# Adding the last two experts' rows after the final norm instead of before it, in a routed feed-forward block on one Trainium2 core

## The chip, the cores and the metric

The program runs on one core of a Trainium2 chip. The metric is device microseconds (us) of one execution, less being better. TensorE is called PE, VectorE DVE, ScalarE ACT, GpSimd POOL; SyncE (SP) and POOL issue the DMAs spoken of here.

## What is computed

The reference is one layer (a convolution and recurrence mixer, a cross-attention, a mixture of experts) and a final norm. Only its end matters here:

```python
def rms_norm(x, g):
    y = x * lax.rsqrt(jnp.mean(x * x, axis=-1, keepdims=True) + 1e-6)
    return y * g

# 1024 tokens of 1024 numbers; 16 experts in 4 groups of 4
# a token takes ONE group, and two experts of that group
for e in range(16):
    hid = silu(t @ w_gate[e]) * (t @ w_up[e])          # 1024 -> 512
    out = out + combine[:, e:e+1] * (hid @ w_down[e])  # 512 -> 1024
x = x + out
return rms_norm(x, final_norm)                         # row by row
```

## The kernel before

Float32 products are made of three products of the high and low parts of both operands, so every weight tile is split once: a cast on ACT (`split_hi`, L163) and a subtraction on DVE (`split_lo`, L169).

**Routing.** `idi` and `wts` hold, for every expert, the token numbers and gates of its first 128 rows (`slot(e, 0)`) and of up to 64 further rows (`slot(e, 1)`). Blank places hold numbers of 1024 and more, which the scatters skip. What the further rows need stands under `second(e)`, a branch on a flag of the expert, taken by PE, ACT and DVE. `ORDER` runs through the groups in turn, so that the last two experts, `p` and `LAST` (numbers 11 and 15), belong to different groups: no token has both. In the run profiled here the flag is set for `p`, not for `LAST`.

**The sum.** `acd` is a DRAM copy of the residual rows. An expert's rows are added to it by an indirect accumulating DMA from POOL (`add_rows`, L1200), first rows and further rows apart. Each such DMA touches `acd` at places that the program doesn't know when it is built, so each waits until the one before has landed.

**The weights.** `Weights` (`X`) streams the tiles. Nine raw slots take loads from SP, in the order in which W was filled; `X.split(n)` splits up to n tiles into free slots out of 14 pairs, and each split frees a raw slot and issues the next load. `X.get` splits until the wanted tile is there. All of this part is in `manual_schedule`: every engine runs its instructions in the order of the code.

**The loop** (L1323) takes expert `e`: gate and up products (`gate_up`, L1327, 48 matmuls of 128x512), `hidden`, the down products of the expert before (`down`, 24 matmuls), its scaled rows (`weighted`, L1148) and scatter-add, `over` (turns the hidden rows for the next down product), the further rows of the expert before, `over2`, `turned2`.

**The tail** (L1368 to L1425) has the down products of `p`, its two scatter-adds, the gate and up products of `LAST`, its `hidden`, reads of all eight 128-row tiles of `acd` (L1403, SP), and the down products of `LAST`.

**The final phase** (L1429 to L1484) places the rows of `LAST` by matmuls with one-hot matrices (L1437, L1443). Even tiles (mode A) are added on DVE (L1450), squared on ACT (L1459), and scaled on DVE (L1467). In odd tiles (mode B) a matmul with the identity adds the residual (L1445), ACT squares out of PSUM (L1456), DVE scales (L1470). POOL makes the reciprocal root (L1457, L1460, L1461), SP stores each tile (L1475).

Of the kernel before, what the change touches and what calls it, by code (L numbers as in the profile page):

```python
# [8 lines left out]
F32 = mybir.dt.float32  # L9
F32R = mybir.dt.float32r  # L10
# [43 lines left out]
C_N = C_WR + ND * 24  # L54


MODES = "ABABABAB"
START = 12
FILL = 2
LAG = 2  # L60


class Slots:
# [22 lines left out]
def block_kernel(ctx: ExitStack, tc: tile.TileContext, A):  # L86
# [572 lines left out]
    for s, e in enumerate(ORDER):  # L659
        gu = [("gu", e, k) for k in range(ND)]  # L660
        dn = [("dn", ORDER[s - 1], k) for k in range(4)] if s else []
        for name, i, k in dn + gu if s == NE - 1 else gu + dn:
            W.add((name, i, k), A["w_" + name][i, k])
    for k in range(4):
        W.add(("dn", ORDER[-1], k), A["w_dn"][ORDER[-1], k])
# [541 lines left out]
    def second(e):  # L1207

        return tc.If((flags & (1 << e)) > 0, preferred_fallthrough_block=True)

    hrow = [half.get() for _ in range(2)]
    routed = half.get(BF16, (P, P))
    act.copy(routed, idf)
# [98 lines left out]
    with tc.manual_schedule():  # L1312
        flags = nc.values_load(two[0:1, 0:1], engines=(PE, ACT, DVE), min_val=0, max_val=(1 << NE) - 1)
        X = Weights(W.jobs, W.flying, W.ready, RAW)
        X.load()
        x0 = x0_bufs[0]
        run(turned(x0, xg[0]))
        with second(ORDER[0]):
            turned2()
        for i in range(2):  # L1320
            fetch(ORDER[1], i)
        pool.memset(og[1][LO], 0.0)
        for s, e in enumerate(ORDER[:-1]):  # L1323
            p = ORDER[s - 1] if s else None
            nx = ORDER[s + 1]
            for k in range(ND):
                gate_up(x0, X.get(("gu", e, k)), k)  # L1327
                X.split(1)
            hidden()
            ws = [X.get(("gu", e, k)) for k in range(ND)]  # L1330
            with second(e):
                for k in range(ND):
                    gate_up2(ws[k], k)
                hidden2(slot(e, 1)[1])
            for k in range(ND):
                X.drop(("gu", e, k))
            x0 = x0_bufs[(s + 1) % 2]
            ops = turned(x0, xg[0])
            if s + 2 < NE:
                fetch(ORDER[s + 2], 0)  # L1340
            run(ops)
            X.split(2)
            if p is not None:
                wd = [X.get(("dn", p, k)) for k in range(4)]
                for k in range(4):
                    down(wd[k], k)
                X.split(1)
                weighted(slot(p, 0)[1])
                add_rows(slot(p, 0)[0], og[0])
            over()  # L1350
            X.split(2)
            if p is not None:
                with second(p):
                    for k in range(4):
                        down2(wd[k], k)
                    rows2(og[1])
                add_rows(slot(p, 1)[0][LO], og[1][LO])
                for k in range(4):
                    X.drop(("dn", p, k))
            with second(e):  # L1360
                over2()
            with second(nx):  # L1362
                turned2()
            if s + 2 < NE:
                fetch(ORDER[s + 2], 1)


        p, LAST = ORDER[-2:]  # L1368
        wd = [X.get(("dn", p, k)) for k in range(4)]
        for k in range(4):  # L1370
            down(wd[k], k)
        X.split(1)
        weighted(slot(p, 0)[1])
        add_rows(slot(p, 0)[0], og[0])
        with second(p):
            for k in range(4):
                down2(wd[k], k)
            rows2(og[1])
        add_rows(slot(p, 1)[0][LO], og[1][LO])
        for k in range(4):  # L1380
            X.drop(("dn", p, k))
        slots.put(*xg, *x0_bufs[NE % 2])
        fn, row = slots.get(), slots.get()
        oh = slots.get(F32R), slots.get(F32R)
        pool.iota(row, pattern=[[1, T]], base=0, channel_multiplier=0, allow_small_or_imprecise_dtypes=True)
        pool.dma_start(fn, A["final_norm"])
        for k in range(ND):
            gate_up(x0, X.get(("gu", LAST, k)), k)
            X.split(2)
        hidden()  # L1390
        ws = [X.get(("gu", LAST, k)) for k in range(ND)]
        with second(LAST):
            for k in range(ND):
                gate_up2(ws[k], k)
            hidden2(slot(LAST, 1)[1])
        for k in range(ND):
            X.drop(("gu", LAST, k))
        assert not X.jobs
        X.split(4)
        wd = [X.get(("dn", LAST, k)) for k in range(4)]  # L1400
        acc = [X.place(X.raw, F32) for _ in range(NT)]
        for t in range(NT):
            sp.dma_start(acc[t], acd[cut(t), :])  # L1403
        over()
        with second(LAST):
            over2()
        slots.put(*x0, xp)
        slots.free.extend(X.raw)
        ogs = [[slots.get(F32R) for _ in range(2)] for _ in range(2)]
        for i in range(2):  # L1410
            dve.tensor_scalar(oh[i], row, idf[:, LAST * 8 + i:LAST * 8 + i + 1], None, op0=ALU.is_equal)
        with second(LAST):
            for k in range(4):
                down2(wd[k], k)
            rows2(og[1])
            split(ogs[1][0][LO], ogs[1][1][LO], og[1][LO])
        for k in range(4):
            down(wd[k], k)
        for n in range(2):
            split(ogs[0][0][:, HS[n]], ogs[0][1][:, HS[n]], dn_banks[n], slot(LAST, 0)[1])  # L1420
        for k in range(4):
            X.drop(("dn", LAST, k))
        slots.free.extend(X.pair)
        slots.put(*og, hid, hp)
        banks.put(*gu_banks, *dn_banks, *turn_banks)  # L1425

    ssf = const.tile([P, 2 * NT], F32, name="ssf")  # L1429
    rf = const.tile([P, NT], F32, name="rf")  # L1430
    pss, jk = {}, {}

    def placed(t):
        jk[t] = slots.get()
        pss[t] = [banks.get() for _ in range(2)]
        for n, ps in enumerate(pss[t]):
            pe.matmul(ps, oh[0][:, cut(t)], ogs[0][0][:, HS[n]], start=True, stop=False)  # L1437
        with second(LAST):
            for n, ps in enumerate(pss[t]):
                for o in ogs[1]:  # L1440
                    pe.matmul(ps, oh[1][LO, cut(t)], o[LO, HS[n]], start=False, stop=False)
        for n, ps in enumerate(pss[t]):
            pe.matmul(ps, oh[0][:, cut(t)], ogs[0][1][:, HS[n]], start=False, stop=MODES[t] != "B")  # L1443
            if MODES[t] == "B":
                pe.matmul(ps, ident, acc[t][:, HS[n]], start=False, stop=True)  # L1445

    def added(t):
        if MODES[t] != "B":
            for n, ps in enumerate(pss[t]):
                dve.tensor_tensor(acc[t][:, HS[n]], ps, acc[t][:, HS[n]], op=ALU.add)  # L1450

    def summed(t):
        r, s2 = rf[:, t:t + 1], [ssf[:, 2 * t + n:2 * t + n + 1] for n in range(2)]
        if MODES[t] == "B":
            for n, ps in enumerate(pss[t]):
                act.activation(jk[t][:, HS[n]], ps, AF.Square, scale=1.0 / 32.0, accum_out=s2[n])  # L1456
            pool.tensor_scalar(r, s2[0], s2[1], EPS, op0=ALU.add, op1=ALU.add)  # L1457
        else:
            act.activation(jk[t], acc[t], AF.Square, scale=1.0 / 32.0, accum_out=s2[0])  # L1459
            pool.tensor_scalar(r, s2[0], EPS, None, op0=ALU.add)  # L1460
        pool.tensor_tensor(r, r, mhalf[:, 0:1], op=ALU.pow)  # L1461
        slots.put(jk[t])

    def scaled(t):
        r = rf[:, t:t + 1]
        if MODES[t] == "A":
            dve.scalar_tensor_tensor(acc[t], acc[t], r, fn, op0=ALU.mult, op1=ALU.mult)  # L1467
        elif MODES[t] == "B":
            for n, ps in enumerate(pss[t]):
                dve.scalar_tensor_tensor(acc[t][:, HS[n]], ps, r, fn[:, HS[n]], op0=ALU.mult, op1=ALU.mult)  # L1470
        else:
            act.activation(acc[t], acc[t], AF.Copy, scale=r)
            pool.tensor_tensor(acc[t], acc[t], fn, op=ALU.mult)
        banks.put(*pss[t])
        sp.dma_start(A["out"][cut(t), :], acc[t])  # L1475

    with tc.manual_schedule():
        for t in range(NT + LAG):
            if t < NT:
                placed(t)  # L1480
                added(t)
                summed(t)
            if t >= LAG:
                scaled(t - LAG)  # L1484


def layout(inputs):
# [63 lines left out]
```

## Time and profile before

| | |
|---|---|
| median of the runs | 1223.09 us (1222.92 to 1223.41) |
| the profiled execution | 1224.64 us, its span 1222.9 us |
| PE busy over the span | 96% |
| DVE, ACT, POOL busy | 58%, 46%, 15% |
| mean granted clock of PE | 0.988 of full speed |

A busy share is a mean over a span with several stages. The stages around the change are the last 66 us, from 1157 us on; the two loops of stages ahead of them are not touched but for the one split named below. The time of an execution is 1.7 us more than its span.

### The profile page before, as it was taken

Reading aid. Unit: us, or ns where it says so; the run is one execution under the profiler, and the core shown is the slowest. Engines: PE = TensorE matmul, PEld = TensorE weight load, DVE = VectorE, ACT = ScalarE, POOL = GpSimd, SP = SyncE. Lnnn points to the kernel's source line nnn. Section 1 sums busy time; section 2 is a strip of 40 time slices with the busy share of each in tenths; the row PEclk is TensorE's granted clock in tenths of the full one; section 3 lists DMA queues with packets and bytes.
Section 4 is the critical chain, followed back from the end, with each engine's and each line's share of the span. In section 5 each row is a group of like instructions: output and inputs, shape, how many; then the busy total and the mean of one; then the engine's idle time right before and its main releaser. Section 6 shows DMA issues by size and latency. Waiting matters only on the chain. (4 is left out here: it accounts for less than half of the span.)

```text
span 1222.9 us, 20592 instructions
## 1 busy us (share of the span) xinstructions
PE 1178.0 (96%) x7918; PEld 966.8 (79%) x7918; DVE 712.3 (58%) x1162; ACT 567.5 (46%) x965; POOL 188.6 (15%) x229
## 2 busy tenths in 40 slices
PE   9999999999999999999999999789999999999985
PEld 7787878787889988898888888568787777787762
DVE  6625454547457512364454776756867768668645
ACT  6613232323335402463244443545866767658633
POOL 1100101010100100100001333212223222123122
PEclk9999999999999999999999999889999999999988
DMA  9601110111426811120032321667979779798764
GB/s 343 240 18 48 41 54 35 36 53 54 157 85 242 281 63 35 35 104 1 1 121 83 125 104 70 218 232 242 317 245 377 254 263 349 255 338 290 247 176 194
DMA packets 58316, 196.48 MB, mean 161 GB/s; under 512 B 8925, under 2 KB 9565, under 8 KB 58208
## 3 DMA queue, kind: packets, MB, share of 16 engines
q1 hardware_dynamic: 45216, 157.69, 35.2%
q0 software_dynamic: 12704, 37.26, 10.4%
q8 instruction: 68, 1.11, 0.4%
q14 instruction: 40, 0.33, 0.1%
q10 hardware_dynamic: 288, 0.09, 0.0%
HBM read 173.49 MB, written 29.62 MB: 166 GB/s over the span
## 5 line engine op out<-in xcount | busy, mean ns | idle before, releaser
L257 PE MATMUL b<-s,s 128*128 128x512 f32 (+1 forms) x1056 | 402.7, 382 | 0.9 <-ACT s L165 0.8
L259 PE MATMUL b<-s,s 128*128 128x512 f32 (+1 forms) x1056 | 392.6, 372 | 0.0
L258 PE MATMUL b<-s,s 128*128 128x512 f32 (+1 forms) x1056 | 392.1, 371 | 0.1
L169 DVE TENSOR_TENSOR s<-s,s 128x1024 fp32r<-128x1024 f32 (+2 forms) x272 | 315.1, 1203 | 57.1 <-ACT s L163 35.4
L163 ACT CAST s<-s 128x1024 fp32r<-128x1024 f32 (+2 forms) x272 | 268.2, 1042 | 133.5 <-PE b L259 47.7
L1124 PE MATMUL b<-s,s 128*128 128x512 f32 x1152 | 275.3, 397 | 4.5 <-PEq L1362 1.7
L1124 PEld LDWEIGHTS b<-s,s 128*128 128x128 f32 x1152 | 217.0, 191 | 51.9 <-ACT s L163 2.7
L259 PEld LDWEIGHTS b<-s,s 128*128 128x128 f32 x1056 | 199.0, 188 | 35.4 <-issue 0.2
L257 PEld LDWEIGHTS b<-s,s 128*128 128x128 f32 x1056 | 199.0, 189 | 33.5 <-ACT s L165 1.5
L258 PEld LDWEIGHTS b<-s,s 128*128 128x128 f32 x1056 | 199.5, 189 | 31.3 <-DVE s L171 1.0
L169 DVE TENSOR_TENSOR s<-b,s 128x512 fp32r<-128x512 f32 (+1 forms) x112 | 70.9, 647 | 45.5 <-ACT s L163 42.5
L1200 POOL DMA_INDIRECT acd<-s,idi x30 | 59.2, 1972 | 204.9 <-ACT s L1148 66.4
L1163 PE MATMUL b<-s,s 128*128 128x512 f32 x384 | 90.5, 391 | 0.0
L1163 PEld LDWEIGHTS b<-s,s 128*128 128x128 f32 x384 | 71.6, 188 | 14.7
L163 ACT CAST s<-b 128x512 fp32r<-128x512 f32 (+1 forms) x112 | 60.7, 558 | 42.6 <-PE b L264 16.6
L1106 POOL DMA_INDIRECT s<-h3d,idi x32 | 37.1, 1160 | 106.4 <-PE b L1114 87.3
L1175 ACT COPY h<-b 64x512 f32<-64x512 f32 x32 | 18.6, 582 | 67.7 <-PE b L1163 57.0
L1176 DVE TENSOR_TENSOR h<-b,h 64x512 f32<-64x512 f32 x16 | 10.9, 682 | 63.1 <-ACT h L1175 63.1
L784 DVE TENSOR_TENSOR s<-b,s 128x512 f32<-128x512 f32 x16 | 11.0, 691 | 58.7 <-PE b L259 58.6
L264 PE MATMUL b<-ident,s 128*128 128x128 f32 x288 | 40.9, 273 | 1.0 <-DVE s L615 0.9
L547 DVE TENSOR_TENSOR s<-s,s 128x512 f32<-128x512 f32 x28 | 19.3, 691 | 37.6 <-PE b L538 22.1
L264 PEld LDWEIGHTS b<-ident,s 128*128 128x128 f32 x288 | 34.5, 140 | 8.0 <-DVE s L615 1.3
(232 smaller groups left out, 920.2 us busy)
## 6 DMA issues: line engine op xcount, KB each, us to landing
s<-in_w_gu_dram SPq DMA_DIRECT2D x128, 512.0 KB, 6.8
s<-in_w_dn_dram SPq DMA_DIRECT2D x64, 512.0 KB, 7.5
s<-in_w_in_dram SPq DMA_DIRECT2D x26, 512.0 KB, 3.5
s<-in_w_kv_dram SPq DMA_DIRECT2D x16, 512.0 KB, 5.5
h3d<-s POOLq DMA_DIRECT2D x9, 512.0 KB, 3.1
acd<-s POOLq DMA_DIRECT2D x9, 512.0 KB, 3.2
s<-in_xT_dram SPq DMA_DIRECT2D x16, 256.0 KB, 5.5
s<-in_x_dram SPq DMA_DIRECT2D x8, 512.0 KB, 9.0
```

Source lines behind the costliest of these rows:

```text
L163: act.copy(hi, src)
L169: (eng or dve).tensor_tensor(lo, src, hi.bitcast(F32), op=ALU.subtract)
L257: pe.matmul(ps, lh, rh, start=first, stop=False)
L258: pe.matmul(ps, lh, rl, start=False, stop=False)
L259: pe.matmul(ps, ll, rh, start=False, stop=last)
L264: pe.transpose(pt[:, cut(c)], src[:, cut(half * 4 + c)], ident)
L547: dve.tensor_tensor(k4[:, :, 0, :], k4[:, :, 0, :], tv[:, :, 1:2].to_broadcast([P, nb, w]), op=ALU.mult)
L1106: pool.indirect_dma_start(out=to, out_offset=None, in_=h3d, in_offset=rows, bounds_check=T - 1, oob_is_err=False)
L1124: pe.matmul(ps[n], l, r[:, HS[n]], start=a, stop=b)
L1163: pe.matmul(ps[n], l, r[:, HS[n]], start=first and i == 0, stop=last and i == 1)
L1175: act.copy(up2[UP], ps[UP])
L1200: pool.indirect_dma_start(out=acd, in_=src, in_offset=None, compute_op=ALU.add, out_offset=rows, bounds_check=T - 1, oob_is_err=False)
```

## The change

The down products of `p` move behind the gate and up products of `LAST`; the weights come in that order too. In the loop's last turn, the two splits between `over` and the second scatter-add of expert 7 are left out there, and their tiles are split later.

The rows of `p` and `LAST` are no longer added to `acd`. All eight tiles of `acd` are read as they are after expert 7 (four into free slots, four into raw slots as these come free during the products of `LAST`), normed and stored to the output: tiles 0 to 2 ahead of `over`, tiles 3 to 7 behind the further rows of `p`. The rows that `p` and `LAST` change are gathered from `acd` by four indirect DMAs of POOL. Each expert's products are added to its rows (`first_sum`, `second_sum`), the sum is normed, and stored over the output's rows by an indirect DMA (`store`), which skips blank places. Gone are the one-hot placing and its operands, the identity matmuls, and the two scatter-adds of `p`. Odd tiles change from mode B to mode C: ACT scales by the root, POOL multiplies by the norm's weights.

```diff
-MODES = "ABABABAB"
+MODES = "ACACACAC"
...
-        for name, i, k in dn + gu if s == NE - 1 else gu + dn:
+        for name, i, k in gu + dn:
...
             over()
-            X.split(2)
+            if nx != ORDER[-1]:
+                X.split(2)
...
         p, LAST = ORDER[-2:]
-        wd = [X.get(("dn", p, k)) for k in range(4)]
-        for k in range(4):
-            down(wd[k], k)
-        X.split(1)
-        weighted(slot(p, 0)[1])
-        add_rows(slot(p, 0)[0], og[0])
-        with second(p):
-            for k in range(4):
-                down2(wd[k], k)
-            rows2(og[1])
-        add_rows(slot(p, 1)[0][LO], og[1][LO])
...
+        def residual(ts):
+            for t in ts:
+                sp.dma_start(acc[t], acd[cut(t), :])
+
+        def root(r, *ss):
+            if len(ss) == 2:
+                pool.tensor_scalar(r, ss[0], ss[1], EPS, op0=ALU.add, op1=ALU.add)
+            else:
+                pool.tensor_scalar(r, ss[0], EPS, None, op0=ALU.add)
+            pool.tensor_tensor(r, r, mhalf[0:r.shape[0], 0:1], op=ALU.pow)
...
+        def scaled(t):
+            r = rf[:, t:t + 1]
+            if MODES[t] == "A":
+                dve.scalar_tensor_tensor(acc[t], acc[t], r, fn, op0=ALU.mult, op1=ALU.mult)
+            else:
+                act.activation(acc[t], acc[t], AF.Copy, scale=r)
+                pool.tensor_tensor(acc[t], acc[t], fn, op=ALU.mult)
+            sp.dma_start(A["out"][cut(t), :], acc[t])
+
+        def final(ts):
+            for i, t in enumerate(ts):
+                summed(t)
+                if i:
+                    scaled(ts[i - 1])
+            scaled(ts[-1])
...
+        def first_sum(j, e):
+            a, (r, ss) = ax[j][0], again(j, 0)
+            for n in range(2):
+                dve.scalar_tensor_tensor(a[:, HS[n]], dn_banks[n], slot(e, 0)[1], a[:, HS[n]],
+                                         op0=ALU.mult, op1=ALU.add)
+                squares(a[:, HS[n]], ss[n])
+            root(r, *ss)
+
+        def second_sum(j, e, wd):
+            a, (r, ss) = ax[j][1][LO], again(j, 1)
+            with second(e):
+                for k in range(4):
+                    down2(wd[k], k)
+                rows2(og[1])
+                dve.tensor_tensor(a, a, og[1][LO], op=ALU.add)
+                squares(a, ss[0][LO])
+            root(r[LO], ss[0][LO])
+
+        def store(ix, src):
+            rows = bass.IndirectOffsetOnAxis(ap=ix, axis=0)
+            pool.indirect_dma_start(out=A["out"], in_=src, in_offset=None, out_offset=rows,
+                                    bounds_check=T - 1, oob_is_err=False)
+
+        def first_out(j, e):
+            a, r = ax[j][0], again(j, 0)[0]
+            dve.scalar_tensor_tensor(a, a, r, fn, op0=ALU.mult, op1=ALU.mult)
+            store(slot(e, 0)[0], a)
+
+        def second_out(j, e):
+            a, r = ax[j][1][LO], again(j, 1)[0]
+            with second(e):
+                dve.scalar_tensor_tensor(a, a, r[LO], fn[LO], op0=ALU.mult, op1=ALU.mult)
+            store(slot(e, 1)[0][LO], a)
...
         for k in range(ND):
             gate_up(x0, X.get(("gu", LAST, k)), k)
-            X.split(2)
+            X.split(1)
+            if not X.jobs and len(X.raw) >= 5 and len(acc) == 4:
+                residual(range(4))
+                acc += [X.place(X.raw, F32) for _ in range(4)]
+                residual(range(4, NT))
+                fn = X.place(X.raw, F32)
+                pool.dma_start(fn, A["final_norm"])
...
         X.split(4)
-        wd = [X.get(("dn", LAST, k)) for k in range(4)]
-        acc = [X.place(X.raw, F32) for _ in range(NT)]
-        for t in range(NT):
-            sp.dma_start(acc[t], acd[cut(t), :])
+        wd, wl = ([X.get(("dn", e, k)) for k in range(4)] for e in (p, LAST))
+        slots.free.extend((*X.pair, *X.raw))
+        jk = slots.get()
+        ax = [[slots.get() for _ in range(2)] for _ in range(2)]
+        for j, e in enumerate((p, LAST)):
+            for i in range(2):
+                ix, to = (slot(e, 1)[0][LO], ax[j][1][LO]) if i else (slot(e, 0)[0], ax[j][0])
+                pool.indirect_dma_start(out=to, out_offset=None, in_=acd,
+                                        in_offset=bass.IndirectOffsetOnAxis(ap=ix, axis=0))
+        final(range(0, 3))
+        for k in range(4):
+            down(wd[k], k)
         over()
+        first_sum(0, p)
+        second_sum(0, p, wd)
         with second(LAST):
             over2()
+        final(range(3, NT))
+        first_out(0, p)
+        second_out(0, p)
+        second_sum(1, LAST, wl)
+        second_out(1, LAST)
         for k in range(4):
+            down(wl[k], k)
+        first_sum(1, LAST)
+        first_out(1, LAST)
```

## Rows read from the trace of the kernel before

**Rows 1.** The page's 40 slices of the span (30.6 us each): busy tenths of PE.

```profile
PE   9999999999999999999999999789999999999985
```

**Rows 2.** Instructions of PE in order of time, merged (start, length, line, operation, count; in brackets the idle time before and what ended it): the 48 gate and up products of expert 7, the 24 down and 16 further-row products of `p`, the 48 gate and up products of `LAST`, the turn of its hidden rows, its 24 down products.

```profile
1107.55 11.16 PE L1124 MATMUL b<-s,s 128*128 128x512 f32 x48 [0.27 <-PEq L1362]
...
1157.14 5.95 PE L1124 MATMUL b<-s,s 128*128 128x512 f32 x24 [0.42 <-ACT s L163]
...
1162.93 3.79 PE L1163 MATMUL b<-s,s 128*128 128x512 f32 x16
...
1166.56 5.60 PE L1124 MATMUL b<-s,s 128*128 128x512 f32 x24
...
1173.07 0.73 PE L1124 MATMUL b<-s,s 128*128 128x512 f32 x2 [0.91 <-ACT s L163]
...
1174.33 5.28 PE L1124 MATMUL b<-s,s 128*128 128x512 f32 x22 [0.53 <-DVE s L169]
...
1182.87 1.12 PE L1139 MATMUL b<-ident,h 128*128 128x128 f32 x4 [3.26 <-DVEq L1392]
...
1184.71 7.73 PE L1124 MATMUL b<-s,s 128*128 128x512 f32 x24 [0.72 <-ACTq L1405]
```

**Rows 3.** POOL and SP in order of time, merged: the last four scatter-adds (expert 7, first and further rows; `p`, first and further rows), and the reads of `acd`.

```profile
1156.89 2.15 POOL L1200 DMA_INDIRECT acd<-s,idi  x1 [15.51 <-ACT s L1148]
1167.85 1.43 POOL L1200 DMA_INDIRECT acd<-s,idi  x1 [8.81 <-DMA acd<-s,idi]
1171.11 1.56 POOL L1200 DMA_INDIRECT acd<-s,idi  x1 [1.82 <-DMA acd<-s,idi]
1178.00 2.12 POOL L1200 DMA_INDIRECT acd<-s,idi  x1 [5.33 <-DVE s L169]
...
1183.53 5.05 SPq L1403 DMA_DIRECT2D s<-acd  x8
```

**Rows 4.** DMA issues (KB each, median us from issue to landing), one answer for the window of each of the four scatter-adds above, in the same order; then the first two reads of `acd` and the last one; the last store of the output; a gather of 128 rows (`h3d`) at 775.5 us.

```profile
acd<-s,idi POOLq DMA_INDIRECT x1, 10.2
...
acd<-s,idi POOLq DMA_INDIRECT x1, 2.5
...
acd<-s,idi POOLq DMA_INDIRECT x1, 6.2
...
acd<-s,idi POOLq DMA_INDIRECT x1, 5.2
...
s<-acd SPq DMA_DIRECT2D x2, 512.0 KB, 6.0
...
s<-acd SPq DMA_DIRECT2D x1, 512.0 KB, 10.1
...
out_dram<-s SPq DMA_DIRECT2D x1, 512.0 KB, 2.7
...
s<-h3d,idi POOLq DMA_INDIRECT x1, 4.6
```

**Rows 5.** The final phase in order of time, merged: PE's first two one-hot products and SP's last store.

```profile
1193.00 1.07 PE L1437 MATMUL b<-s,s 128*128 128x512 f32 x2 [0.55 <-ACT s L165]
...
1215.06 0.33 SPq L1475 DMA_DIRECT2D out_dram<-s  x1
```

**Rows 6.** Splits of seven weight tiles in a row, ACT and DVE in order of time, merged; and ACT's two splits that the change takes out of the loop's last turn, and its step of `over2` of `p` behind them.

```profile
1110.42 6.75 ACT L163 CAST s<-s 128x1024 fp32r<-128x1024 f32 x7 [0.17 <-ACTq L1362]
...
1112.06 8.04 DVE L169 TENSOR_TENSOR s<-s,s 128x1024 fp32r<-128x1024 f32 x7 [0.29 <-DVEq L1362]
...
1156.96 2.03 ACT L163 CAST s<-s 128x1024 fp32r<-128x1024 f32 x2
1159.32 0.37 ACT L1157 CAST s<-b 128x256 fp32r<-128x256 f32 x1 [0.33 <-ACTq L1353]
```

**Rows 7.** Groups of instructions by line and shape (busy us, mean ns of one, idle time before and what ended it): square and its read-out on ACT, copy of 64 rows on ACT, the DVE operations that answer to those of the change, the root's two steps and a multiplication of 128x512 on POOL.

```profile
L1459 ACT ACTIVATE s<-s 128x1024 f32<-128x1024 f32 x4 | 4.2, 1057 | 7.7 <-DVE s L1450 6.0 <-issue 1.8
...
L1459 ACT ACTIVATION_READ_ACCUMULATOR s<-s 128x1 f32 x4 | 0.7, 186 | 0.0
...
L1175 ACT COPY h<-b 64x512 f32<-64x512 f32 x32 | 18.6, 582 | 67.7 <-PE b L1163 57.0 <-DVE s L1176 10.6
...
L1176 DVE TENSOR_TENSOR s<-b,h 64x512 f32<-64x512 f32 x16 | 10.9, 683 | 13.7 <-DMA acd<-s,idi 7.9 <-ACTq L1360 4.9 <-ACT h L1175 0.7
...
L1470 DVE SCALAR_TENSOR_TENSOR s<-b,rf,s 128x512 f32<-128x512 f32 x8 | 5.6, 745 | 0.8 <-POOL rf L1461 0.8
...
L1467 DVE SCALAR_TENSOR_TENSOR s<-s,rf,s 128x1024 f32<-128x1024 f32 x4 | 5.1, 1276 | 0.0
...
L961 POOL TENSOR_TENSOR s<-s,s 128x512 f32<-128x512 f32 x8 | 10.4, 1302 | 8.3 <-ACT s L960 8.3
...
L1461 POOL TENSOR_TENSOR rf<-rf,mhalf 128x1 f32<-128x1 f32 x8 | 4.5, 565 | 0.7
...
L1460 POOL TENSOR_SCALAR rf<-ssf 128x1 f32<-128x1 f32 x4 | 0.9, 222 | 21.3 <-ACT s L1459 21.3
```

**Rows 8.** POOL's first step of the root in two odd tiles, and the DVE instruction beside the second of them, in order of time.

```profile
1207.48 0.30 POOL L1457 TENSOR_SCALAR rf<-ssf 128x1 f32<-128x1 f32 x1 [0.60 <-ACT s L1456]
...
1211.50 1.28 DVE L1467 SCALAR_TENSOR_TENSOR s<-s,rf,s 128x1024 f32<-128x1024 f32 x1
...
1211.82 1.13 POOL L1457 TENSOR_SCALAR rf<-ssf 128x1 f32<-128x1 f32 x1 [0.55 <-ACT s L1456]
```

More of the change, by code (lines that the diff above doesn't have):

```diff
@@ L54 @@
 C_N = C_WR + ND * 24
-MODES = "ABABABAB"
+MODES = "ACACACAC"
 START = 12
 FILL = 2
-LAG = 2
 class Slots:
@@ L1209, in second @@
         return tc.If((flags & (1 << e)) > 0, preferred_fallthrough_block=True)
+    ssf = const.tile([P, NT + 8], F32, name="ssf")
+    rf = const.tile([P, NT + 4], F32, name="rf")
+    pool.memset(ssf, 1.0)
     hrow = [half.get() for _ in range(2)]
@@ L1368, in block_kernel @@
         p, LAST = ORDER[-2:]
-        wd = [X.get(("dn", p, k)) for k in range(4)]
-        for k in range(4):
-            down(wd[k], k)
-        X.split(1)
-        weighted(slot(p, 0)[1])
-        add_rows(slot(p, 0)[0], og[0])
-        with second(p):
-            for k in range(4):
-                down2(wd[k], k)
-            rows2(og[1])
-        add_rows(slot(p, 1)[0][LO], og[1][LO])
-        for k in range(4):
-            X.drop(("dn", p, k))
-        slots.put(*xg, *x0_bufs[NE % 2])
@@ L1383, in block_kernel @@
[L1383 to L1386, printed above, removed]
+        assert p // 4 != LAST // 4
+        slots.put(*xg, *x0_bufs[NE % 2])
+        acc = [slots.get() for _ in range(4)]
+        def residual(ts):
[7 more added lines that the diff above has]
+            pool.tensor_tensor(r, r, mhalf[0:r.shape[0], 0:1], op=ALU.pow)
@@ new lines, in squares, with summed @@
+        def squares(a, ss):
+            act.activation(jk[0:a.shape[0], 0:a.shape[1]], a, AF.Square, scale=1.0 / 32.0, accum_out=ss)
+        def summed(t):
+            squares(acc[t], ssf[:, t:t + 1])
+            root(rf[:, t:t + 1], ssf[:, t:t + 1])
+        def scaled(t):
[6 more added lines that the diff above has]
+            sp.dma_start(A["out"][cut(t), :], acc[t])
@@ new lines, in final, with again @@
+        def final(ts):
[4 more added lines that the diff above has]
+            scaled(ts[-1])
+        def again(j, i):
+            c = NT + 2 * j + i
+            return rf[:, c:c + 1], [ssf[:, NT + 4 * j + 2 * i + n:NT + 4 * j + 2 * i + n + 1] for n in range(2)]
+        def first_sum(j, e):
[5 more added lines that the diff above has]
+            root(r, *ss)
@@ L1390, in block_kernel @@
+        assert not X.jobs and len(acc) == NT
         hidden()
@@ L1397, in block_kernel @@
             X.drop(("gu", LAST, k))
-        assert not X.jobs
         X.split(4)
-        wd = [X.get(("dn", LAST, k)) for k in range(4)]
-        acc = [X.place(X.raw, F32) for _ in range(NT)]
-        for t in range(NT):
-            sp.dma_start(acc[t], acd[cut(t), :])
+        wd, wl = ([X.get(("dn", e, k)) for k in range(4)] for e in (p, LAST))
[7 more added lines that the diff above has]
+                                        in_offset=bass.IndirectOffsetOnAxis(ap=ix, axis=0))
@@ L1404, in block_kernel @@
+        final(range(0, 3))
+        for k in range(4):
+            down(wd[k], k)
         over()
+        first_sum(0, p)
+        second_sum(0, p, wd)
         with second(LAST):
             over2()
[L1407 to L1416, printed above, removed]
@@ L1417, in block_kernel @@
-        for k in range(4):
[L1418 to L1484, printed above, removed]
+        final(range(3, NT))
[3 more added lines that the diff above has]
+        second_out(1, LAST)
+        for k in range(4):
+            down(wl[k], k)
+        first_sum(1, LAST)
+        first_out(1, LAST)
 def layout(inputs):
```

## The prediction

> **What bounds the kernel now.** I read the slices of the page first, then PE in order of time, then the DMAs of the last 66 us. PE is at nine tenths in all slices but two until the last two, where it falls to 8 and 5 [rows 1]: ahead of the tail the kernel is bound by PE, and the change adds nothing there. So only the tail is summed, from 1157.1 us on.
>
> In the tail two other things set the pace. First, the scatter-adds stand in a row. Expert 7's first rows take 10.2 us to land beside weight loads, its further rows, all blank, 2.5, those of `p` 6.2 and 5.2, and each starts when the one before has landed [rows 3, 4]. The reads of `acd` start only at 1183.5, and PE's gate and up products of `LAST` and its down products have stalls between them [rows 2, 3]. Second, the final phase runs from 1193.0 to the landing of the last store, 1215.1 + 2.7 = 1217.8 [rows 4, 5]; after it come 5.1 us of the program's end, up to 1222.9.
>
> **Products.** The change takes the down products of `p` and their scatter-adds from in front of `LAST`'s gate and up products. These 48 take 11.2 us where weights are there [rows 2]. By the order of loads and splits, five of their eight tiles are split when the tail begins. The two splits taken out (2.0 us of ACT) let `over2`'s step on ACT come at about 1157.4 instead of 1159.3 [rows 6]. From 1158.1 eight splits follow at 0.96 us on ACT and 1.15 on DVE [rows 6]: the sixth tile is ready at 1160.4 on DVE, and needed at 1157.2 + 7 = 1164.2. So PE ends these products at 1168.4 instead of 1179.6, and the down products of `p` at about 1174.5, its further rows at 1179. **Eleven us come free on PE, and cost nothing on ACT and DVE**, which have the same splits in all. Three splits are left behind `hidden`, done on ACT at 1172.4. If a tile came late here, PE would wait, but the next paragraph has 4 us in hand.
>
> **Reads.** The eight reads no longer wait for the scatter-adds of `p`, only for expert 7's: 1167.85 + 2.5 = 1170.4 instead of 1183.5 [rows 3, 4]. The first read landed 6.0 after its issue, the last 10.1 after an issue at 1188.0, so the eight came 1.2 us apart. Now the norm's weights (0.5 MB) and four gathers, whole 128 or 64 rows each (1.6 MB), run beside 4.2 MB of reads: 1.8 us apart. ACT therefore gets tiles 0, 1 and 2 at 1177.0, 1178.8 and 1180.6, after idling from 1172.4. The gathers go out on POOL behind the scatters, at most 1.5 us each, and land before 1184, where the first is needed.
>
> **From the reads to the last five tiles.** On ACT a square takes 1.06 + 0.19 = 1.25 us [rows 7], so three of them end at 1181.9; the copy of tile 1 (1.06, as a square without its read-out) ends at 1183.0; `over`'s cast (0.6, as a copy out of PSUM) at 1183.6 [rows 7]. DVE scales tile 2 (1.28) to 1184.2, finishes `over` at 1184.9, and adds the first rows of `p` in two halves of 0.75 [rows 7] to 1186.4; ACT squares the second half to 1187.2. The further rows of `p` go to and fro: branch 0.4 (0.33 in a row), copy 0.58, sum 0.68, copy 0.58, sum 0.68, addition 1.2 (a subtraction of such rows 1.15), square 1.25 [rows 6, 7], some 0.8 of handovers and leaving: 6.2 us. **At 1193.4 ACT begins the last five tiles**, so no sooner than the old final phase began. The norm of three tiles is hidden by the products, that of five is not.
>
> Five squares, three copies and three multiplications on POOL follow. A multiplication of 128x1024 is two of 1.30 less a start, 2.55, and a root 0.22 + 0.1 + 0.57 = 0.9 [rows 7]. POOL is the slower of the two: counted from 1193.4, the first copy ends at 3.55, its multiplication at 6.2, root 5 at 7.15, copy 5 at 8.25, its multiplication at 10.85, root 7 at 11.8, copy 7 at 12.95, its multiplication at 15.6. The store lands 0.1 + 2.7 later: 18.4, or 1211.8.
>
> POOL has no such multiplication beside DVE in the trace. The nearest row is a root's first step, which took 1.13 instead of 0.30 us and ended just behind a scaling on DVE that had started before it [rows 8]. Two to four scalings meet POOL's work here, at between 0 and 1.3 us each. I take 2.0 (two at the row's 0.8, and a bit), with 0 and 3.5 as ends: **1213.8**. The Trainium skill ("SBUF — State Buffer", section "Who interferes with whom") says that a DVE instruction with two SBUF inputs and a GpSimd instruction that reads SBUF block each other fully. By that rule every meeting costs up to the whole 1.28 us, and the sum would be 1.5 us later; the row agrees in one case.
>
> **The stores over the output.** An indirect store may touch any row of the output, so it has to wait for the eight stores of tiles, as the scatter-adds to `acd` wait [rows 3], and I take it that the four wait for each other too. POOL runs in order, so behind a waiting store stand the next stores and the last root. A plain scatter isn't in the trace. The nearest rows are the gather of 128 rows at 4.6, the store of a tile at 2.7, an empty scatter at 2.5, scatter-adds of 6.2 and 5.2 when little else runs [rows 4]. I take 4.5 for 128 rows and 3.8 for the further rows of `p`, with 2.5 to 2.7 and 5.2 to 6.2 as ends. Then: `p`'s first rows 0.2 + 4.5; its further rows 0.2 + 3.8; `LAST`'s further rows, all blank, 0.2 + 1.45 on POOL, and behind them in its queue the root of `LAST`'s first rows (0.95), the scaling on DVE (0.1 + 1.28), 0.2 to the next issue; `LAST`'s first rows 4.5. Together 17.4, between 12.5 and 22.2. The last row lands at 1231.2, the span ends 5.1 later at 1236.3. The down products of `LAST` and their sum, done by 1208, are hidden under this.
>
> **The sum.** 1236.3 - 1222.9 = 13.4 us more. On the profiled execution, 1224.6, that is 1238.0; the median of the runs stands 1.5 below it, so 1223.1 + 13.4 = **1236**. Gone are 24.8 us of final phase (1193.0 to 1217.8); in their place come 20.4 for five tiles and 17.4 for four stores in a row. The 11 us that PE gains buy nothing, because PE's last product isn't what ends last. With the ends (lock 0 to 3.5, stores 12.5 to 22.2) the forecast's own range is 1229 to 1243.
>
> The Trainium skill ("DMA: Bandwidth & Descriptors", section "Anatomy of one DMA — SWDGE (gpsimd) path") gives such a DMA about 2.0 us fixed and its bytes at 436 GB/s. As an estimate from that page, 128 rows would take 3.2 us, and the sum would come out some 3 us lower. The empty scatter's 2.5 agrees with the fixed part; no row shows a plain scatter of full rows.
>
> **Rivals.** (1) *The four stores wait for the tiles but not for each other.* For it: they touch no row twice that matters. Against: the scatter-adds of one queue did wait for each other [rows 3]. Then three issues in 5.2, root, scaling and handovers 2.6, last store 4.5: 1213.8 + 12.3 + 5.1 = 1231.2 of span, a time of 1231. The same page of the skill ("Two DMAs through the same engine are not ordered") speaks against this one.
>
> (2) *Not slower: indirect DMAs are slow only beside other loads.* Expert 7's first scatter took 10.2 us while loads ran, `p`'s 6.2 when they were done [rows 4], and the change moves two loads behind it. Were it to land in 6.2, at 1163, the reads would start at 1165.8 and ACT's last split, 1172.4, would set the start: squares, copy, `over`, sums lead to 1187.6 instead of 1193.4. With the stores at their lower ends as well and POOL free of DVE: 1187.6 + 18.4 + 12.5 + 5.1 = 1223.6, a time of 1224, no change; a little less on any of the terms gives faster. It decides when scatter and stores together give back the 13.4 us. Against: most of the loads that ran beside that scatter are still there, and the four links of the chain stay.
>
> (3) *The rows come late*: reads and gathers share the rings worse than I take it, or the change doesn't do what it says, and no tile is normed during the products. Three tiles more behind 1193.4 cost 3 x 1.25 + 2.55 = 6.3: 1242.
>
> **Chances.** Forecast 0.62; rival 1 0.14; rival 2 0.16 (faster 0.08, no change 0.08); rival 3 0.08. A measurement of this kernel can tell about 0.2% (2.4 us) from no change. Faster 0.09, the same 0.09, slower 0.82. For eight in ten the range reaches down to rival 2's time and up to the forecast's end: 1224 to 1243.
>
> **What the profile would show.** Right: PE's 48 products of `LAST` without a gap, ended near 1168; the first read of `acd` near 1170; ACT idle before the first square; the square of tile 3 near 1193; POOL's three multiplications longer than 2.55 where DVE scales; POOL waiting for DMA of the output three times after the last tile's store; the last root on POOL behind these waits. Wrong: if the reads start well ahead of 1170, if the four stores go out without waits between, if a plain scatter lands in under 3 us, or if ACT gets to tile 3 before 1188.

## The result and the profile after

The changed kernel takes 1241.28 us (median of four, 1239.22 to 1241.44) where the kernel before took 1223.25: the ratio is 1.0143, with an interval of 1.0125 to 1.0160. It is slower, as forecast, and 5 us above the 1236 of the forecast.

| | before | after |
|---|---|---|
| profiled execution, its span | 1224.64, 1222.9 | 1239.22, 1237.4 |
| PE busy, its mean granted clock | 96%, 0.988 | 94%, 0.973 |
| POOL busy | 15% | 17% |
| first scatter-add of expert 7 starts | 1156.89 | 1156.89 |
| from there to the end of the span | 66.0 | 80.5 |

Both profiled executions reach the tail at the same time, so the whole difference between these two lies in the tail. Nine later traces reach this point between 1154.5 and 1158.5 us. The last line of the table is therefore the measure by which runs are compared below; for short, the tail's length.

The stages of the tail after, as busy time of each engine in a stretch (count in brackets), then granted clock, DMA share and GB/s:

```profile
1157.00:1172.00 15.00, 14.83 (x64) 12.04 (x65) 13.67 (x14) 11.72 (x14) 4.91 (x3) 1.00 0.75 211
1172.00:1192.40 20.40, 12.76 (x45) 9.80 (x44) 8.39 (x10) 8.71 (x16) 11.71 (x14) 0.75 0.98 335
1192.40:1214.80 22.40, 2.05 (x9) 1.34 (x8) 8.45 (x6) 10.31 (x17) 15.39 (x15) 0.64 0.39 156
1214.80:1230.00 15.20, 0.00 (x0) 0.00 (x0) 1.28 (x1) 0.00 (x0) 5.72 (x8) 0.50 0.22 80
1230.00:1237.40 7.40, 0.00 (x0) 0.00 (x0) 0.00 (x0) 0.00 (x0) 0.00 (x0) 0.50 0.00 0
```

PE (first pair of numbers) is full for 15 us, busy for 12.8 of the next 20.4, and all but idle in the last 45. Its work was brought forward, and nothing came forward behind it. Its granted clock falls to 0.50, the lower of its two levels (1.2 and 2.4 GHz), once it has nothing to do. Here is PE in order of time:

```profile
1157.02 11.14 PE L1123 MATMUL b<-s,s 128*128 128x512 f32 x48 [0.29 <-PEq L1365]
1168.32 5.69 PE L1123 MATMUL b<-s,s 128*128 128x512 f32 x24
1173.85 0.60 PE L1138 MATMUL b<-ident,h 128*128 128x128 f32 x4
1174.20 3.90 PE L1162 MATMUL b<-s,s 128*128 128x512 f32 x16
1185.73 8.72 PE L1123 MATMUL b<-s,s 128*128 128x512 f32 x24 [7.64 <-DVE s L1419]
```

The 48 products of `LAST` have no gap and end at 1168.2; in [rows 2] they ended at 1179.6. The last 24 down products take 8.7 us where those of `p` took 5.7, beside a lower granted clock; they end at 1194, and DVE begins the sum that needs them only at 1207.6, so the clock costs nothing here. 43 us of the span follow. In them POOL sets the pace; here it is in order of time, from its multiplication for tile 3 on:

```profile
1195.91 3.37 POOL L1401 TENSOR_TENSOR s<-s,s 128x1024 f32<-128x1024 f32 x1 [0.15 <-ACT s L1400]
...
1201.50 3.22 POOL L1401 TENSOR_TENSOR s<-s,s 128x1024 f32<-128x1024 f32 x1 [0.30 <-ACT s L1400]
1204.80 1.08 POOL L1385 TENSOR_SCALAR rf<-ssf 128x1 f32<-128x1 f32 x1
1205.96 1.46 POOL L1386 TENSOR_TENSOR rf<-rf,mhalf 128x1 f32<-128x1 f32 x1
1208.68 2.35 POOL L1401 TENSOR_TENSOR s<-s,s 128x1024 f32<-128x1024 f32 x1 [1.26 <-ACTq L1426]
1214.80 1.09 POOL L1436 DMA_INDIRECT out_dram<-s,idi  x1 [3.77 <-issue]
1219.05 0.94 POOL L1436 DMA_INDIRECT out_dram<-s,idi  x1 [3.16 <-issue]
...
1223.01 0.98 POOL L1436 DMA_INDIRECT out_dram<-s,idi  x1 [2.07 <-DMA out_dram<-s,idi]
...
1226.64 1.05 POOL L1436 DMA_INDIRECT out_dram<-s,idi  x1 [1.61 <-DVE s L1441]
```

The stores over the output start 3.8 us behind the last tile's multiplication and go out 4.25, 3.96 and 3.63 us apart. Where a wait is put down to "issue", the profile names no releaser. The landings, one answer for each store in order, show what the waits are for:

```profile
out_dram<-s,idi POOLq DMA_INDIRECT x1, 3.5
...
out_dram<-s,idi POOLq DMA_INDIRECT x1, 3.2
...
out_dram<-s,idi POOLq DMA_INDIRECT x1, 2.0
...
out_dram<-s,idi POOLq DMA_INDIRECT x1, 3.4
```

The second and the third store start 0.75 us behind the landing of the one before. The fourth starts 1.6 us behind the landing of the blank one: it waits for DVE's scaling, and that for the root that stands in POOL's queue behind the blank store. The last store lands at 1230.0. The span ends 7.4 us later, where 5.1 were forecast.

What happens there is seen in the closing DRAIN of POOL, an instruction that the traces show in every engine's queue at the end of the program (shortest, median and longest in ns; first and last start), first before, then after:

```profile
L1547 POOLq DRAIN  x3: 46/109/9029, 1213.0 to 1222.6; - x3
```

```profile
L1557 POOLq DRAIN  x3: 46/109/10203, 1226.4 to 1237.2; - x3
```

The long one begins when POOL's last instruction does, or 0.2 us ahead of it, and ends at 1222.1 before and at 1236.6 after, some 0.8 us ahead of the end of the span. Counted from the end of POOL's last instruction (1213.6 and 1227.7) that is 8.5 and 8.9 us. In the kernel before it outlasts the last landing (1217.8) by 4.3 us. So in neither kernel does a landing set the end.

### The profile page after: what moved, and what is told of

The parts are those of the page before. It is cut to its first block, busy times and chain, and to the rows that moved or that the text cites. A ratio compares the mean times of both kernels' runs of the same rounds, so it can differ in the third digit from the quotient of the medians.

```text
span 1237.4 us, 20491 instructions
## 1 busy us (share of the span) xinstructions
PE 1161.1 (94%) x7870; PEld 958.7 (77%) x7870; DVE 709.6 (57%) x1150; ACT 572.8 (46%) x967; POOL 209.7 (17%) x247
## 5 line engine op out<-in xcount | busy, mean ns | idle before, releaser
L1199 POOL DMA_INDIRECT acd<-s,idi x28 | 55.3, 1974 | 195.8 <-ACT s L1147 73.7
L1174 ACT COPY h<-b 64x512 f32<-64x512 f32 x32 | 18.6, 582 | 66.3 <-PE b L1162 57.0
```

The source lines that it names most:

```text
L1174: act.copy(up2[UP], ps[UP])
L1199: pool.indirect_dma_start(out=acd, in_=src, in_offset=None, compute_op=ALU.add, out_offset=rows, bounds_check=T - 1, oob_is_err=False)
```

## The experiments

**The four stores left out.**

```diff
         def store(ix, src):
             rows = bass.IndirectOffsetOnAxis(ap=ix, axis=0)
-            pool.indirect_dma_start(out=A["out"], in_=src, in_offset=None, out_offset=rows,
-                                    bounds_check=T - 1, oob_is_err=False)
```

> The changed kernel without its four indirect stores over the output: the rows of p and LAST keep the norm without these two experts; all other instructions stay. Theory A (the four stores in a row behind the last tile set the end, and what follows the last row is set by POOL: its closing DRAIN took 9.0 us before and 10.2 after, ending about 8.7 us behind POOL's last instruction in both): the last multiplication on POOL ends near 1211, two roots behind it near 1213, the span ends near 1213 + 8.7 = 1221.5, some 16 us less than 1237.4. Theory B (the end follows the last landing by the 5.1 us of the prediction): last store lands near 1214, span 1219. Rival (the stores are not what ends last): span stays within 2 us of 1237.

The span of the one execution was 1222.4, the tail 65.9 us: 14.6 less than after, and as long as before (66.0). Without the four stores the whole loss is gone. The span didn't end 5 us behind the last tile's landing near 1214 either. POOL's last root ended at 1213.0, its long DRAIN at 1221.6:

```profile
L1555 POOLq DRAIN  x3: 46/109/9191, 1212.4 to 1222.1; - x3
```

Theory A holds on both counts.

**All tiles in mode A.**

```diff
-MODES = "ACACACAC"
+MODES = "AAAAAAAA"
```

> The changed kernel with every tile in mode A: DVE scales all eight, POOL multiplies nothing. If the last five tiles are bound by POOL's multiplications and its port shared with DVE (three of 3.4, 3.2 and 2.4 us), then from 1192.5 five squares of 1.2, a root 0.9, a scaling 1.3 and the store 2.8 land at 1203.6 instead of 1213.8, the chain of four stores follows unchanged (about 4.2 + 4.0 + 3.6 apart), and the span falls by about 10 us to 1227. If only the blocking by DVE counts and not the multiplications themselves, about 3.5 us less. If ACT's squares or the reads of acd bound that phase: under 2 us less.

Ratio 1.0083 (1.0062 to 1.0103), 1233.9 us; the tail 74.4 us, 6.1 less than after. That is neither 10 nor 3.5. All of it lies ahead of the stores: the first goes out 51.8 us behind the first scatter-add instead of 57.9. The multiplications were a pace, but a second one came up behind them. POOL's roots of tiles 5 and 6, in order of time, and the scalings of tiles 4 and 5 on DVE:

```profile
1197.62 1.31 POOL L1385 TENSOR_SCALAR rf<-ssf 128x1 f32<-128x1 f32 x1
1199.02 0.57 POOL L1386 TENSOR_TENSOR rf<-rf,mhalf 128x1 f32<-128x1 f32 x1
1199.68 1.32 POOL L1385 TENSOR_SCALAR rf<-ssf 128x1 f32<-128x1 f32 x1
```

```profile
1197.58 1.28 DVE L1398 SCALAR_TENSOR_TENSOR s<-s,rf,s 128x1024 f32<-128x1024 f32 x1 [0.77 <-POOL rf L1386]
1199.63 1.28 DVE L1398 SCALAR_TENSOR_TENSOR s<-s,rf,s 128x1024 f32<-128x1024 f32 x1 [0.77 <-POOL rf L1386]
```

A first step of 0.22 us [rows 7] takes 1.31, ending when the scaling that began just ahead of it ends. DVE then waits 0.77 for the root. The two engines take turns, 2.05 us for a tile.

**POOL quiet at the end of the kernel before.** The roots of its last two tiles go to ACT and DVE:

```diff
+        act.activation(warm, ones[:, 0:1], AF.Sqrt)
...
-        pool.tensor_tensor(r, r, mhalf[:, 0:1], op=ALU.pow)
+        if t < NT - 2:
+            root(t, pool)
...
+        if eng is pool:
+            pool.tensor_tensor(r, r, mhalf[:, 0:1], op=ALU.pow)
+        else:
+            act.activation(r, r, AF.Sqrt)
+            dve.reciprocal(r, r)
 
     def scaled(t):
         r = rf[:, t:t + 1]
+        if t >= NT - 2:
+            root(t, dve)
```

> The kernel before, with the roots of tiles 6 and 7 made by ACT (Sqrt, its table loaded where ACT idles) and DVE (reciprocal) instead of POOL, so that POOL's last instruction ends near 1208.4 instead of 1213.6; the last store lands 0.5 to 1 us sooner. Theory A (the end is set by POOL's closing DRAIN, some 8.7 us behind its last instruction): POOL is done near 1217, the last landing near 1217 sets the end, the span ends near 1218 to 1219, 4 to 5 us faster than before. Theory B (the end follows the last landing by 5.1 us): 0.5 to 1 us faster.

Ratio 0.9970 (0.9960 to 0.9980), 1219.9 us: faster than both kernels. The tail is 61.4 us, 4.6 less than before. POOL's last instruction ends at 1205.0, its DRAIN at 1213.4; the span ends at 1215.9, 0.9 us after SP has seen the last landing (its first DRAIN starts at 1215.0). Some 1.1 us of the 4.6 were won ahead of the final phase, which starts that much sooner behind the first scatter-add in this execution. The end:

```profile
L1561 POOLq DRAIN  x3: 46/109/9031, 1204.4 to 1215.6; - x3
L1561 SPq DRAIN  x3: 7/7/7, 1215.0 to 1215.3; - x3
```

**POOL kept busy at the end of the kernel before.**

```diff
+        late = slots.get()
+        for i in range(4):
+            pool.memset(late, float(i))
```

> The kernel before, with four fills of a 128x1024 tile (0.96 us each) put at the end of POOL's queue; nobody reads them, and POOL ends near 1217.5 instead of 1213.6, no later than the last store lands (1217.8). Theory A (closing DRAIN of POOL behind its last instruction): the span grows by 3.5 to 4 us. Theory B (the end follows the last landing): no change, within 0.5 us.

Ratio 1.0032 (1.0022 to 1.0043), 1227.9 us; the tail 69.2 us, 3.2 more than before.

```profile
1213.39 3.98 POOL L1487 MEMSET s<- 128x1024 f32 x4
...
L1550 POOLq DRAIN  x3: 46/109/9394, 1216.4 to 1226.4; - x3
```

POOL's last instruction ends 3.8 us later than before, at 1217.4, and the span grows by that less 0.6, though nobody reads what the fills write. With the run above this settles the end: it is the later of POOL's last instruction + 8.4 to 9.0 us (all eleven traces) and the last landing, and then 0.8 or 0.9 us.

**The two splits put back.**

```diff
-            if nx != ORDER[-1]:
-                X.split(2)
+            X.split(2)
```

> The changed kernel with the two splits put back between the turn of the hidden rows and the second scatter-add in the loop's last turn. Theory: that scatter-add waits for the landing of the one before it (1167 us), not for ACT or DVE, and the reads of acd wait for it; so the place of the two splits changes nothing: within 1 us of the changed kernel (about 1.4% over before). Rival (the splits moved behind do bring the scatter-add and with it the reads forward): 2 us or more slower than the changed kernel.

Ratio 1.0151 (1.0135 to 1.0166) beside 1.0143 (1.0125 to 1.0160) after; the tail 81.0 us beside 80.5. This part of the change does nothing that can be measured; the next run shows that two tails can differ by 2 us with the same instructions.

**The blank store issued twice.**

```diff
             store(slot(e, 1)[0][LO], a)
+            if j:
+                store(slot(e, 1)[0][LO], a)
```

> The changed kernel with the store of LAST's further rows, all blank, issued twice. If each store over the output waits for the landing of the one before, 3.0 to 4.0 us slower than the changed kernel (the blank store lands 2.0 us after its issue; the last store's scaling, now hidden under the second blank store, gives back some of it: 3.0 is the likeliest). If the stores only wait for the tiles and follow each other on POOL: 1.3 us at most.

Ratio 1.0156 (1.0137 to 1.0174): the intervals overlap, the time alone tells nothing. The tail is 85.1 us, 4.6 more than after, but 2.2 of these were lost before the first store, behind a read that landed late: ACT's square of tile 2 begins 26.2 us behind the first scatter-add instead of 24.0. The rest lies in the stores. From the third on, POOL in order of time:

```profile
1223.24 0.98 POOL L1436 DMA_INDIRECT out_dram<-s,idi  x1 [2.06 <-DMA out_dram<-s,idi]
1225.55 0.91 POOL L1436 DMA_INDIRECT out_dram<-s,idi  x1 [1.34 <-DMA out_dram<-s,idi]
...
1229.12 1.06 POOL L1436 DMA_INDIRECT out_dram<-s,idi  x1 [1.61 <-DVE s L1441]
```

The additional store waits for the landing of the blank one, 2.3 us after its issue, and the last store comes 5.9 us after the third instead of 3.6. So the stores wait for each other, and a link costs a landing even if it moves no row. I had put the additional one at 3.0 to 4.0; it is 2.3.

**Roots off POOL.** As mode A alone, and every root on ACT and DVE, as in the run with POOL quiet. The call of `root` also moves, from `summed` to `scaled`.

```diff
-MODES = "ACACACAC"
+MODES = "AAAAAAAA"
...
-                pool.tensor_scalar(r, ss[0], EPS, None, op0=ALU.add)
-            pool.tensor_tensor(r, r, mhalf[0:r.shape[0], 0:1], op=ALU.pow)
+                dve.tensor_scalar(r, ss[0], EPS, None, op0=ALU.add)
+            act.activation(r, r, AF.Sqrt)
+            dve.reciprocal(r, r)
...
         def summed(t):
             squares(acc[t], ssf[:, t:t + 1])
-            root(rf[:, t:t + 1], ssf[:, t:t + 1])
 
         def scaled(t):
             r = rf[:, t:t + 1]
+            root(r, ssf[:, t:t + 1])
```

> The changed kernel with all tiles in mode A and every root made by ACT (Sqrt) and DVE (sum, reciprocal) instead of POOL, so that POOL does nothing in the tail but its indirect DMAs. Against the run with mode A alone: there the first step of a root on POOL took 1.3 us instead of 0.22 beside DVE's scalings, 2.05 us from tile to tile. If this blocking is the pace, tiles now follow in 1.45 us, the last tile lands 3 to 4 us sooner, and the last store no longer waits for a root that stands in POOL's queue behind other stores (1.6 us): 4 to 6 us less than that run, a span of 1226 to 1228. If ACT or the reads are the pace, only the 1.6 us.

Ratio 1.0083 (1.0067 to 1.0098), no better than mode A alone; tail 73.8 beside 74.4. The gain that I forecast did not come. POOL no longer blocks anything, but the first step of a root now stands behind the scaling of the tile before in DVE's own queue, where the moved call puts it, 1.82 us from tile to tile instead of 2.05. DVE in order of time, two scalings and the step between them:

```profile
1197.17 1.28 DVE L1399 SCALAR_TENSOR_TENSOR s<-s,rf,s 128x1024 f32<-128x1024 f32 x1
1198.37 0.15 DVE L1385 TENSOR_SCALAR rf<-ssf 128x1 f32<-128x1 f32 x1
...
1198.98 1.28 DVE L1399 SCALAR_TENSOR_TENSOR s<-s,rf,s 128x1024 f32<-128x1024 f32 x1
```

Even these 0.9 us for four tiles were lost again, since the first of the last five scalings began 1.4 us later behind the first scatter-add. Whether tiles would follow in 1.45 us with the roots in another place of DVE's queue was not tried. The last store goes out 2.7 us after the third instead of 3.6: 0.9 less, not 1.6, because it still waits for the blank store's landing.

**The changed kernel mended.** As the run above, with another order, and a branch around the stores of further rows:

```diff
-            store(slot(e, 1)[0][LO], a)
+            with tc.If((flags_p & (1 << e)) > 0, preferred_fallthrough_block=True):
+                store(slot(e, 1)[0][LO], a)
...
-        final(range(0, 3))
+        act.activation(warm, ones[:, 0:1], AF.Sqrt)
         for k in range(4):
             down(wd[k], k)
         over()
+        final(range(0, 4))
         first_sum(0, p)
         second_sum(0, p, wd)
         with second(LAST):
             over2()
-        final(range(3, NT))
+        second_sum(1, LAST, wl)
+        for k in range(4):
+            down(wl[k], k)
+        final(range(4, NT))
+        first_sum(1, LAST)
         first_out(0, p)
         second_out(0, p)
-        second_sum(1, LAST, wl)
         second_out(1, LAST)
-        for k in range(4):
-            down(wl[k], k)
-        first_sum(1, LAST)
         first_out(1, LAST)
```

> As the run with roots off POOL, and besides: the turn of LAST's hidden rows ahead of the tiles, four tiles ahead of p's sums instead of three, LAST's down products and sums ahead of the last four tiles and of all stores, and the stores of further rows inside a branch of POOL on the expert's flag, so that LAST's blank one isn't issued. Theory (last tile's landing, then a chain of stores that each wait for the landing of the one before, then POOL's closing DRAIN of about 9 us behind its last instruction): last tile lands near 1201.5, three stores about 4.2 and 4.0 apart, the last issued by 1211, end near 1220: within 0.3% of the kernel before, either side. Rival (the end is not tied to POOL's last instruction but to the last landing by 5.1 us): last row lands 1213.5, end 1218.6.

Ratio 1.0077 (1.0064 to 1.0091), the tail 75.4: my forecast for this run was 12 us too low. Three stores went out, 5.0 and 4.0 apart, and the end came 9.7 us behind POOL's last instruction, as the theory has it, so the end is right and the links nearly. What was wrong is the landing of the last tile: its store goes out at 1208.4, where the landing was forecast for 1201.5. ACT's squares of tiles 0 to 3, in order of time:

```profile
1175.76 1.06 ACT L1390 ACTIVATE s<-s 128x1024 f32<-128x1024 f32 x1 [0.59 <-DMA s<-acd]
...
1178.08 1.06 ACT L1390 ACTIVATE s<-s 128x1024 f32<-128x1024 f32 x1 [1.17 <-DMA s<-acd]
...
1182.07 1.06 ACT L1390 ACTIVATE s<-s 128x1024 f32<-128x1024 f32 x1 [2.74 <-DMA s<-acd]
...
1184.93 1.06 ACT L1390 ACTIVATE s<-s 128x1024 f32<-128x1024 f32 x1 [1.62 <-DMA s<-acd]
```

The tiles come 2.3 to 4.0 us apart; each of these squares waits for its read. DVE scales the fourth tile only at 1188.2 and goes on to `p`'s sums at 1189.4, which is 4.0 us later behind the first scatter-add than in the run with roots off POOL; the last four tiles begin at 1199.0. The run changes several things at once, and none of them was tried by itself.

**The kernel before without two waits.** The trace of before has ACT waiting 6.3 us and DVE 7.9 us for expert 7's scatter-adds to land, because the rows of `p` go into the tiles that these still read:

```profile
1167.21 1.27 ACT L1148 ACTIVATE s<-b,wts 128x512 f32<-128x512 f32 x2 [6.30 <-DMA acd<-s,idi]
...
1170.59 0.68 DVE L1176 TENSOR_TENSOR s<-b,h 64x512 f32<-64x512 f32 x1 [7.88 <-DMA acd<-s,idi]
```

The edit, without the part on the roots, which is that of the run with POOL quiet:

```diff
-        weighted(slot(p, 0)[1])
-        add_rows(slot(p, 0)[0], og[0])
+        for n in range(2):
+            act.activation(xg[0][:, HS[n]], dn_banks[n], AF.Copy, scale=slot(p, 0)[1])
+        add_rows(slot(p, 0)[0], xg[0])
...
-            rows2(og[1])
-        add_rows(slot(p, 1)[0][LO], og[1][LO])
+            rows2(xg[1])
+        add_rows(slot(p, 1)[0][LO], xg[1][LO])
```

> The kernel before with the last two tiles' roots off POOL, and besides: in the tail, the scaled rows of p go into the two gather tiles that are free by then, not into the two tiles that expert 7's scatter-adds still read, so ACT (6.3 us of waiting in the trace of before) and DVE (7.9 us) no longer wait for those to land and split the weights of LAST in time. The scatter-adds themselves still stand in a row and the reads of acd start as before. Theory: PE's products of LAST lose their stalls and its hidden rows come 3 to 5 us sooner; the final phase then starts when the first reads land (6.0 us after their start) instead of behind the products, 3 us sooner: 3 us less than with the roots alone, about 0.5% faster than before. Rival (the reads are what the final phase waits for already): the same as with the roots alone, 0.3% faster.

Ratio 0.9937 (0.9924 to 0.9950), 1215.7 us, the fastest. The tail is 58.1 us, 3.3 less than with the roots alone. The 48 products of `LAST` run in 11.0 us, and the final phase starts 31.7 us behind the first scatter-add, where it starts at 36.1 before [rows 5] and at 35.0 with the roots alone. The 3.3 us between these last two are the whole gain of the tail:

```profile
1166.26 11.04 PE L1124 MATMUL b<-s,s 128*128 128x512 f32 x48
1179.18 0.66 PE L1139 MATMUL b<-ident,h 128*128 128x128 f32 x4 [1.88 <-DVEq L1393]
1180.56 7.20 PE L1124 MATMUL b<-s,s 128*128 128x512 f32 x24 [0.72 <-ACTq L1406]
1188.31 1.08 PE L1439 MATMUL b<-s,s 128*128 128x512 f32 x2 [0.55 <-ACT s L165]
```

## Why the prediction was right, point by point

**PE comes free and it buys nothing.** Forecast: 48 products without a gap until 1168.4. Measured 1168.2. PE isn't what ends last, and without the four stores the tail is no shorter than before.

**The reads.** Forecast from 1170.4, first square at 1177.0. Expert 7's further rows took 4.5 us to land, not 2.5, so the reads began at 1172.4; yet the first square began at 1176.7, since the first read landed within 4.4 us of its issue and not 6.0 [rows 4]. Two errors cancelled here by luck: 2.0 us too early, 1.6 us too long. Expert 7's two scatter-adds, the reads, and ACT's squares of tiles 0 and 3:

```profile
acd<-s,idi POOLq DMA_INDIRECT x1, 9.8
...
1167.46 2.22 POOL L1199 DMA_INDIRECT acd<-s,idi  x1 [8.42 <-DMA s<-in_w_dn_dram]
...
acd<-s,idi POOLq DMA_INDIRECT x1, 4.5
...
1172.36 4.81 SPq L1379 DMA_DIRECT2D s<-acd  x8
...
1176.73 1.06 ACT L1389 ACTIVATE s<-s 128x1024 f32<-128x1024 f32 x1 [5.03 <-DMA s<-acd]
...
1192.46 1.06 ACT L1389 ACTIVATE s<-s 128x1024 f32<-128x1024 f32 x1 [0.17 <-ACTq L1484]
```

**Three tiles hidden, five not.** Forecast for the square of tile 3: 1193.4. Measured 1192.5; the further rows of `p` took 5.3 us to and fro where 6.2 were taken.

**POOL against DVE.** Forecast for the first store: 1214.0, with 2.0 us for blocking. Measured 1214.8. The multiplications took 3.37, 3.22 and 2.35 us where 2.55 was taken, and the steps of the last root 1.08 and 1.46 where they take 0.22 and 0.57 [rows 7]. So the blocking was nearer to 3 us. From the square of tile 3 to the end of the last multiplication it is 18.6 us for 17.6; from there to the first store 3.8 for 3.0. The rule of the Trainium skill ("SBUF — State Buffer", section "Who interferes with whom") that such instructions block each other fully agrees with all of these rows, and with the scaling on DVE that took 3.36 us beside a multiplication on POOL instead of 1.28:

```profile
1202.43 3.36 DVE L1441 SCALAR_TENSOR_TENSOR s<-s,rf,s 128x1024 f32<-128x1024 f32 x1
```

**Four stores in a row.** Forecast 17.2 us from the first issue to the last landing (the 17.4 without the first 0.2). Measured 15.2, with landings of 3.5, 3.2, 2.0 and 3.4. The landings of full rows were taken 1.0 us too long, and the 0.2 from a landing to the next issue 0.55 too short. Rival 1 fell with the waits in the trace and the blank store issued twice. The 3.2 us that come out, as an estimate, of the fit in the Trainium skill ("DMA: Bandwidth & Descriptors", section "Anatomy of one DMA — SWDGE (gpsimd) path") were nearer than my 4.5; its 2.0 fixed is what the blank store took.

**The end.** Here the term was mis-sized, and its mechanism was wrong: 5.1 us behind the last landing were forecast, 7.4 came. In the row that I read it from, POOL's DRAIN ended by chance 4.3 us behind the landing. Because POOL issues the last store, the DRAIN now starts late as well; the term is 8.9 us behind the end of that issue and 0.8 more.

The sum of the span is 1236.3 forecast and 1237.4 measured: the first store +0.8, the stores in a row -2.0, the end +2.3. That it comes within 1.1 us is luck in part, since the last two nearly cancel. The other 4 us between 1236 and the median of 1241.3 aren't in the tail of the profiled execution. Three of the four timed runs lie 2 us above it, the forecast was set against a median 1.5 us below its own profiled execution, and 1223.1 + 13.4 is 1236.5. Which stage makes the runs differ was not tried; the run with the blank store issued twice shows that the reads of `acd` alone can differ by 2.2 us between executions.

Rival 2 had the first scatter-add land sooner: it took 9.8 us instead of 10.2. Rival 3 had the rows late; the first three squares began within 0.9 us of the forecast. In the mended order, which needs a fourth tile sooner, ACT did wait for the reads.

## What to carry to other kernels

Work brought forward on the busiest engine is worth what the last engine's chain lets through: count the links that wait for a landing, 2 us or more each here even when they move nothing. Give POOL its last instruction some 9 us ahead of the last landing; a last store issued by SP, as in the kernel before, isn't enough. Moving two roots off POOL made this kernel 0.3% faster. A tile that a slow DMA still reads holds up whoever writes it next: another buffer gave as much again.

## What had not been expected of the hardware

In all eleven traces a DRAIN of POOL ends 8.4 to 9.0 us behind POOL's last instruction, whether that is a root (8.4 to 8.6), a fill (8.4) or an indirect DMA (8.8 to 9.0). In nine of them the program's end waits for it; in the two with POOL quiet the last landing comes later. In the changed kernel the DMA engines move nothing in the last 6.6 us of this DRAIN. What it does in that time is open.

A store of a tile, 2.7 us in [rows 4], took 13.3 us to land when issued at 1180.2 among the reads and gathers of the changed kernel, where the DMA engines were busy for 0.98 of the time.
